# Two-layer decoder trunk on one core: gate columns joined to a key chunk, compression in two steps, other step orders, another order of the first loads

## The chip, the cores and the metric

The kernel runs on one core of a Trainium2 chip. The metric is the device time of one execution in microseconds (us). The core has TensorE (PE in the profile; its weight loads are PEld), VectorE (DVE), ScalarE (ACT), GpSimd (POOL) and SyncE (SP), which here issues most of the DMA transfers. Before the change the median of three runs is 1027.73 us (1026.06 to 1029.51).

## The reference, cut to what matters

256 tokens of width 1024 pass two layers, and each layer is feed-forward, token mixer, feed-forward:

```python
x = x + 0.5 * swiglu(rmsnorm(x, ffn1_norm[i]), ffn1_w_gu[i], ffn1_w_down[i])
h = rmsnorm(x, mix_norm[i])
y = nsa_mixer(h, ...)  # layer 0
y = swa_mixer(h, ...)  # layer 1
x = x + y
x = x + 0.5 * swiglu(rmsnorm(x, ffn2_norm[i]), ffn2_w_gu[i], ffn2_w_down[i])
```

The mixer of layer 0 (called NSA below) projects `h` to 16 query heads, to three pairs of keys and values of 4 groups, and to 48 gate columns (3 branches by 16 heads). The first pair of keys and values is compressed: overlapping blocks of 32 tokens go through a small two-layer network (`w1`, gelu, `w2`) to 15 coarse keys and values. The queries attend to the coarse keys, to selected blocks and to a window, and the three results are added with `sigmoid(gate columns)` as weights. At this size the selected blocks and the window both come to causal attention over all tokens. The mixer of layer 1 (SWA below) is attention over a window of 128 keys with two key groups and a sink per head. Everything is float32.

## The kernel before

**Weights.** Every weight tile is read in pieces of up to 1024 columns (`Weights.load`, line 166): a DMA issue on SP into a tile `raw` (5 buffers, line 172), a rounded copy `hi` (line 173, mostly ACT) and the rest `lo = raw - hi` (line 179; on DVE in one instruction, on POOL in two of 512 columns). `hi` and `lo` have 4 buffers each. A product is then three matmuls (line 119): `hi` by `hi`, `hi` by `lo`, `lo` by `hi`. In the profile the weights of the NSA projection are called nin, those of its output projection nout, of the compression cmp, of SWA sin and sout, of the feed-forward gu and dn; the suffixes `_r`, `_h`, `_l` are raw, hi and lo.

**Which engine.** The table `ENGINES` (line 45) gives for each kind of helper operation a string over A, V and G (ACT, DVE, POOL); the n-th use takes the n-th letter, from the start again after the end (`pick`, line 145).

**Order.** Feed-forward blocks run in the order written. The mixers are made of steps in a written list (`NSA_STEPS`, line 63, and `SWA_STEPS`, line 70). A step named `X01@n` is step X for group 0 and token tile 1; n is added to its priority while it is laid down (`run`, line 139), and the scheduler fills each engine's queue by priority among what is ready, so a negative n pulls a step ahead. The queues themselves run strictly in order. The steps of NSA: `R` is a block of the input projection (`RowsProduct.block`, line 315), for both token tiles or for one (`R00`, `R01`); its accumulator is a PSUM bank of the kind "acc" (two banks), with `+` of the kind "out" and "sc", with `*` of "sc". Chunk x holds the columns of the keys to be compressed, y those of the values, a to d the other keys and values of a group, 0 to 3 the queries, and g the 48 gate columns, which have a block, a weight piece of 384 columns and accumulators of their own (line 699). `K` (line 723) takes x or y through rope and a transpose into `kc`; `B` (line 588) adds the position codes (`xr`) and splits; `H` (line 603) is the whole compression network; `G` (line 706) turns the gate accumulators into gates, one Tanh on ACT (line 710) and one DVE instruction (line 711) per token tile; `P` and `V` prepare queries and keys; `S` is logits and softmax (lines 480 to 512); `M` weighs the values (line 514); `Q` and `L` are the coarse branch. After the list comes nout. SWA has `R`, `A` (keys), `P`, `S`, `M`, and then sout.

**The start** (`Norm.first`, line 263) has an order written by hand: eight matmuls on zeros, loads of the input x on the queues of SP and ACT, of the identity matrix and of all small parameters, transposes of x (`turn`), their eviction with the gain (`leave`, ACT line 203 and DVE line 206), and the first products as their weight pieces come. The scale of the rows (line 237 to 241) is transposed into `rb` (line 391) before the first gate can be worked out.

Of the kernel before, what the change touches and what calls it, by code (L numbers as in the profile page):

```python
# [44 lines left out]
ENGINES = {  # L45
    "hi_gu": "A", "lo_gu": "V", "hi_dn": "A", "lo_dn": "VGVVVGGV", "hi_nin": "AAAAAVAAAAAAVAAA",
    "lo_nin": "VGGGVGGVVVGGVGVG", "hi_cmp": "A", "lo_cmp": "VVGVVVGVVGGVVVGG", "hi_nout": "AAGAAAAVAVGAVAAA",
    "lo_nout": "VG", "hi_sin": "A", "lo_sin": "GGGGGVVVVGGVGVVG", "hi_sout": "A", "lo_sout": "G",
    "sqh": "GAAVAAAGGAAAGGAA", "sql": "GGGVVVGVGGVGVVVG", "qs": "AVVAVAAAAAAAAAAA", "kdh": "VVVAVGGVGVGAAAAA",
    "kdl": "G", "kk": "A", "ropeadd": "GGGVVGGGVGGGVVGG", "sc1": "VVVVVVVVVVVVVAVV", "sc2": "VVVGVVGVVVVVGVVV",  # L50
    "ph": "A", "tmp": "A", "oh": "A", "ol": "VGVVVGVVGVGVVVVV", "dup": "AVVVAVAGAVVVAVVV", "kca": "AVAAAVVA",
    "kcb": "A", "xr": "VGVV", "xhc": "VVVAGVVAVGVVVVVV", "xlc": "GVGGVGGVGVGVVGGV", "pc": "AAVAAAAAVAVAAAAA",
    "late": "GGGVGGGGGGGGGGGG", "xh": "AAAVVVAVAVAVVVAV", "ga": "G", "g0": "A", "u1": "A", "u0": "G", "hv": "V",
    "hh": "AGVAGVGG", "hl": "GGGGVGGV",
}
# [15 lines left out]
    "R0.+ Rk0@10 P01 Rk1@-40 R10+@-30 A1 P00@20 R11 A0@60 S00 P10 S01 P11 S11@-10 R20 S10 R21+@-20 M00@-20 R30 P20 "  # L71
    "S20 R31@-10 M01@-20 P21@-60 S21@80 M10@20 M11 P30@-10 S30@40 M20 M21 M30@-90 P31@10 S31@80 M31@-210"
# [9 lines left out]

IDLE = 8
# [4 lines left out]
NCP = 16  # L88
KCW = 272
# [9 lines left out]
def trunk_kernel(tc, x_in, wgu, wdn, nsa_in, nsa_w1, nsa_out, swa_in, swa_out, small, fgain, consts, out):  # L99
# [3 lines left out]
    with ExitStack() as es:  # L103
# [46 lines left out]
        def copy(key, o, i):  # L150
            c = pick(key)
# [8 lines left out]
        class Weights:  # L160
# [4 lines left out]

            def load(self, c0, n, pieces=None, engines=None):
                o = c0
                for i, w in enumerate(pieces or [PIECE] * (n // PIECE) + [n % PIECE] * (n % PIECE > 0)):
                    raw = wp.tile([P, PIECE], F32, tag="raw", bufs=BUFS["raw"], name=f"{self.name}_r{o}")
                    hi = wp.tile([P, PIECE], F32R, tag="whi", bufs=BUFS["whi"], name=f"{self.name}_h{o}")  # L170
                    lo = wp.tile([P, PIECE], F32R, tag="wlo", bufs=BUFS["wlo"], name=f"{self.name}_l{o}")
                    self.last = nc.sync.dma_start(raw[:, :w], self.src[:, o:o + w]).ins
                    copy("hi_" + self.kind, hi[:, :w], raw[:, :w])
                    letter = engines[i % len(engines)] if engines else pick("lo_" + self.kind)
                    eng = nc.vector if letter == "V" else nc.gpsimd
                    step = 512 if eng is nc.gpsimd else PIECE
                    for q in range(0, w, step):
                        e = min(w, q + step)
                        eng.tensor_tensor(lo[:, q:e], raw[:, q:e], hi[:, q:e], ALU.subtract)  # L179
                    self.parts[o] = (hi, lo)  # L180
                    o += w
# [62 lines left out]
        class Norm:  # L244
# [18 lines left out]
            def first(self, wts, product):  # L263


                def load_x(h, queues):
                    for t, queue in enumerate(queues):
                        queue.dma_start(x[t][h], x_in[t * P:(t + 1) * P, h * 512:(h + 1) * 512])

                evict = {}  # L270

                def turn(*kps):
                    for kp in kps:
                        evict[kp] = transposed(kp, 0, self.h, self.l, self.both, "A")
# [8 lines left out]
                for _ in range(IDLE):  # L283
                    mm(ps, zeros[:, :P], zeros, True, True)
# [12 lines left out]
                turn(2, 3)  # L297
                product(1, 3)
                leave(4, 6)
                wts.load(1024, 1024, [512, 512], "VG")  # L300
                leave(5, 7)
                product(4, 6, 5, 7)
                wts.load(CHUNK, CHUNK, engines="VG")
                for h in range(2):
                    squares(h, h * 512, h * 512 + 512, self.v, True)
                self.r = row_scale(self.v, "n0")


        class RowsProduct:
# [5 lines left out]
            def block(self, ts=(0, 1), tag=None):  # L315
# [52 lines left out]
        def ffn(i, norm, nxt, residual=Residual):  # L368
            with tc.tile_pool(name=f"ffn{i}", bufs=1) as fp:
# [24 lines left out]
                for f in range(NF):  # L394
# [5 lines left out]
                    if i == 0 and f == 3:  # L400
                        with tc.issue_after(wts.last):
                            nc.sync.dma_start(cst[:, P:], consts[:, P:])
                    g0 = fp.tile([P, S], F32, tag="g0", bufs=BUFS["g0"], name=f"g0{f}")
# [147 lines left out]
        def nsa(norm, nxt):  # L551
            with tc.tile_pool(name="nsa", bufs=1) as mp:
# [50 lines left out]
                def compress(xh, xl):  # L603
                    wts1 = Weights(nsa_w1, "cmp")
                    ps = s_bank("hid")[:, :S]
                    for j in range(16):
# [7 lines left out]
                        mm(ps, xlj, wh, False, j == 15)  # L614
                    a = mp.tile([P, P], F32, name="ge_a")
# [9 lines left out]
                    for r, c in own:  # L625
                        nc.vector.tensor_mul(b[r], ps[r, c], a[r])
                    pt = s_bank("hidT")[:, :P]
# [50 lines left out]
                class Finish:  # L678
# [11 lines left out]
                    def scale(self, sm):  # L690
# [8 lines left out]
                                   [48 if c == "g" else S for c in NSA_CHUNKS], "nin",  # L699
                                   ["out" if c == "g" else "acc" for c in NSA_CHUNKS])  # L700
                xh, xl = {}, {}
# [31 lines left out]
                def step_H():  # L733
                    compress(xh, xl)
# [198 lines left out]
def _pack(i):  # L933
# [16 lines left out]
    nsa_blocks.update(g=[(2560, 2608)], x=[(D, D + S)], y=[(D + S, D + 2 * S)])  # L950
# [39 lines left out]
```

## Time and profile before

| what | value |
|---|---|
| median of 3 runs | 1027.73 us (1026.06 to 1029.51) |
| the profiled execution's own time | 1030.59 us |
| its span in the profile | 1028.8 us |
| PE busy over the span | 991.0 us (96%), 5671 matmuls |
| DVE, ACT, POOL busy | 706.0, 554.6, 525.9 us |
| mean granted TensorE clock | 0.982 of full speed |
| HBM read | 167 MB, 163 GB/s over the span |

The span has these stages: start and first feed-forward 0 to 198 us, NSA 198 to 376, two feed-forwards 376 to 745, SWA 745 to 837, last feed-forward to the end. "Busy" of PE is the time in which at least one matmul is in flight, so a PE that is busy can still go at half its clock, which the column PEclk tells (1.00 is 2.4 GHz, 0.50 is 1.2 GHz). A wait is put down to the instruction that ended it.

### The profile page before, as it was taken

To read this page: it belongs to the slowest core of one execution; us is meant where nothing else is said; L and a number is where in the kernel's file an instruction comes from. 1 tells how busy PE (TensorE), PEld (TensorE's weight loads), DVE (VectorE), ACT (ScalarE), POOL (GpSimd) and SP (SyncE) were. 2 spreads that over 40 slices of the span, in tenths; PEclk is the share of its full clock that TensorE was granted. 3 is DMA by queue.
4 is the path that set the end of the run, shared out by engine and by line. 5 is a ranking of instruction groups with operands and counts; after the bars stand their busy time and mean duration, and the time that the engine had idled before them with its cause. 6 is when DMAs were issued, how large, how long until landed. Compare 5 with 4: busy or idle time off the path is not lost.

```text
span 1028.8 us, 15995 instructions
## 1 busy us (share of the span) xinstructions
PE 991.0 (96%) x5671; PEld 858.3 (83%) x5671; DVE 706.0 (69%) x1294; ACT 554.6 (54%) x1041; POOL 525.9 (51%) x503
## 2 busy tenths in 40 slices
PE   7999999998889999999999999999998999999997
PEld 5888888897778788888888888888887778888897
DVE  5777743468878987777535878764177888778533
ACT  5455544347548845555444555544347855555442
POOL 2776563455453316555631465564575516655643
PEclk9999999989989999999999999999999999999999
DMA  7666665542321256666566566656642256666661
GB/s 260 199 202 200 187 190 178 173 143 83 123 83 29 81 159 183 189 190 192 177 195 202 168 203 184 188 166 219 179 142 73 83 164 194 198 185 188 194 188 42
DMA packets 47599, 169.10 MB, mean 164 GB/s; under 512 B 5280, under 2 KB 5792, under 8 KB 47520
## 3 DMA queue, kind: packets, MB, share of 16 engines
q1 hardware_dynamic: 46512, 166.11, 53.9%
q10 hardware_dynamic: 1008, 1.98, 0.6%
q8 instruction: 44, 0.72, 0.3%
q14 instruction: 35, 0.29, 0.1%
HBM read 167.02 MB, written 1.05 MB: 163 GB/s over the span
## 4 chain that ended last, share of the span: by engine, by line
PE 85%; DVE 6%; POOL 3%; ACT 3%; issue 3%; DMA 1%; SPq 0%; POOLq 0%; DVEq 0%; ACTq 0%
PE gu L119 47%; PE dn L119 23%; PE nin L119 5%; PE nout L119 1%; PE sout L119 1%; PE na_o L119 1%; DVE na_p L511 1%; PE sin L119 1%; PE xt L195 1%; ACT sa_p L507 1%; PE sa_o L119 1%; PE na_t L520 1%; DMA gu_r<-in_wgu_dram 1%; POOL sout_l L179 0%; POOL nin_l L179 0%
## 5 line engine op out<-in xcount | busy, mean ns | idle before, releaser
L119 PE MATMUL gu<-xh,gu_h 128*128 128x512 f32 x1408 | 489.2, 393 | 2.4 <-DVE xh L206 2.4
L119 PE MATMUL gu<-xh,gu_l 128*128 128x256 f32 x1408 | 391.7, 280 | 0.2 <-POOL gu_l L179 0.2
L119 PEld LDWEIGHTS gu<-xh,gu_h 128*128 128x128 f32 x1408 | 263.3, 188 | 60.7 <-DVE xh L206 2.6
L119 PEld LDWEIGHTS gu<-xh,gu_l 128*128 128x128 f32 x1408 | 265.5, 189 | 2.3 <-DVE gu_l L179 0.7
L179 DVE TENSOR_TENSOR gu_l<-gu_r,gu_h 128x1024 fp32r<-128x1024 f32 (+1 forms) x175 | 234.0, 1337 | 27.4 <-ACT gu_h L153 26.8
L153 ACT CAST gu_h<-gu_r 128x1024 fp32r<-128x1024 f32 (+2 forms) x178 | 184.6, 1039 | 38.8 <-PE gu L119 16.8
L153 ACT CAST dn_h<-dn_r 128x1024 fp32r<-128x1024 f32 (+1 forms) x89 | 92.2, 1041 | 105.8 <-PE dn L119 99.6
L119 PE MATMUL dn<-dn_h,hh 128*128 128x512 f32 (+1 forms) x396 | 146.0, 369 | 0.0
L119 PE MATMUL dn<-dn_l,hh 128*128 128x512 f32 (+1 forms) x396 | 145.5, 368 | 0.0
L119 PE MATMUL dn<-dn_h,hl 128*128 128x512 f32 (+1 forms) x396 | 145.1, 366 | 0.0
L179 POOL TENSOR_TENSOR dn_l<-dn_r,dn_h 128x512 fp32r<-128x512 f32 x66 | 90.0, 1386 | 100.2 <-ACT dn_h L153 99.9
L179 DVE TENSOR_TENSOR dn_l<-dn_r,dn_h 128x1024 fp32r<-128x1024 f32 (+1 forms) x56 | 71.3, 1277 | 97.9 <-ACT dn_h L153 97.9
L158 POOL TENSOR_TENSOR ga<-g,rb 128x256 f32<-128x256 f32 x88 | 100.3, 1140 | 61.8 <-DVE g L410 52.2
L158 POOL TENSOR_TENSOR hl<-u,hh 128x256 fp32r<-128x256 f32 x66 | 82.4, 1249 | 50.9 <-ACT hh L153 25.1
L158 POOL TENSOR_TENSOR u<-u,rb 128x256 f32<-128x256 f32 x88 | 68.9, 783 | 60.3 <-DVE u L412 60.3
L414 ACT ACTIVATE th<-ga 128x256 f32<-128x256 f32 x88 | 36.9, 419 | 106.7 <-POOL ga L158 106.2
L119 PEld LDWEIGHTS dn<-dn_h,hl 128*128 128x128 f32 x396 | 74.7, 189 | 12.9
L119 PEld LDWEIGHTS dn<-dn_h,hh 128*128 128x128 f32 x396 | 74.8, 189 | 12.4
L119 PEld LDWEIGHTS dn<-dn_l,hh 128*128 128x128 f32 x396 | 74.8, 189 | 11.9
L119 PE MATMUL nin<-nin_h,xh 128*128 128x256 f32 (+1 forms) x352 | 76.0, 310 | 2.0 <-DVE r_b L443 1.9
L153 ACT COPY g<-gu 128x256 f32<-128x256 f32 x88 | 32.8, 373 | 78.0 <-PE gu L119 77.0
L416 DVE SCALAR_TENSOR_TENSOR ga<-th,ga 128x256 f32<-128x256 f32 x88 | 43.1, 490 | 40.1 <-ACT th L414 40.0
(244 smaller groups left out, 1471.7 us busy)
## 6 DMA issues: line engine op xcount, KB each, us to landing
gu_r<-in_wgu_dram SPq DMA_DIRECT2D x174, 512.0 KB, 4.4
dn_r<-in_wdn_dram SPq DMA_DIRECT2D x87, 512.0 KB, 3.8
nin_r<-in_nsa_in_dram SPq DMA_DIRECT2D x20, 512.0 KB, 3.6
sin_r<-in_swa_in_dram SPq DMA_DIRECT2D x10, 512.0 KB, 3.6
nout_r<-in_nsa_out_dram SPq DMA_DIRECT2D x8, 512.0 KB, 3.6
sout_r<-in_swa_out_dram SPq DMA_DIRECT2D x8, 512.0 KB, 3.7
cmp_r<-in_nsa_w_dram SPq DMA_DIRECT2D x4, 512.0 KB, 4.6
x<-in_x_dram ACTq DMA_DIRECT2D x3, 256.0 KB, 6.0
```

What stands on the lines that cost most here:

```text
L119: nc.tensor.matmul(o, w, m, start=start, stop=stop)
L153: nc.scalar.copy(o, i)
L158: (nc.vector if pick(key) == "V" else nc.gpsimd).tensor_tensor(o, a, b, op)
L179: eng.tensor_tensor(lo[:, q:e], raw[:, q:e], hi[:, q:e], ALU.subtract)
L195: nc.tensor.transpose(ps[:, kk * S + t * P:kk * S + (t + 1) * P], x[t][kp // 2][:, c:c + P], ident)
L414: nc.scalar.activation(th, ga, AF.Tanh, scale=0.5)
L416: nc.vector.scalar_tensor_tensor(ga, th, 1.0, ga, ALU.add, ALU.mult)
L507: nc.scalar.activation(o, o, AF.Exp, bias=mn[:, c:c + 1], scale=-1.0, accum_out=sm[:, c:c + 1])
L511: nc.vector.tensor_tensor(o, o, sm[:, b * 4:b * 4 + 4, None].to_broadcast([P, 4, nk]), ALU.mult)
L520: nc.tensor.transpose(ps[:, hh * P:(hh + 1) * P], pr[:, hh, kt * P:(kt + 1) * P], ident)
```

## The change

1. The 48 gate columns are no chunk of their own. They stand behind the 256 columns of chunk x, which so has 304; `G` reads columns 256 to 303 of x's accumulators. The weight pieces of a block whose width does not divide 1024 are whole rows of tiles: x loads 912, 912 and 608 columns in place of 1024, 1024 and, for g, 384.
2. `compress` ends after the matmuls with `w1`; gelu is `compress_rest`, and transpose and second layer are `compress_out`, a new step `I`, which stands after `P11` in the list.
3. Both lists have another order and other offsets.
4. At the start the identity moves from SP's queue to ACT's, the first two weight pieces are issued on SP right after the first part of x, one part of x moves from ACT to SP behind them, only the first 48 columns of the small parameters are loaded there (the other 240 after the fourth block's weights of the first feed-forward, on SP), three more zero matmuls stand between the first transposes and the first product, and evictions and weight splits take another order.
5. Letters in `ENGINES` change. Those that are used, by use:

```
hi_nin  use 5        V -> A   (1024 columns)
hi_nout use 2        G -> A   (8 uses: AAGAAAAV -> AAAAAAAV)
lo_sin  10 uses      GGGGGVVVVG -> GGGVVVGVVG
lo_sout 8 uses       G -> V
xr      use 2        V -> G   (128x512)
xhc     use 2, 3     V, A -> G, A
dup     use 0        A -> V
ol      16 uses      VGVVVGVVGVGVVVVV -> VVVVVGVGGGGGVVVV
sqh 6: A -> G, sql 8: G -> V, kdh 9: V -> A
```

The diff, cut to its core:

```diff
 NSA_STEPS = (
-    "Ry.+@-40 Rx R00* R01 K00@10 K01 K10 Rg.+ Ra P00 G@80 K11 B0@70 V00@50 P01@-70 V01 R10+@-10 B1 S00 R11 S01 "
-    "H@10 M00 P10 Q0@-60 Rb P11 V10 S10 V11 R20@10 R21@170 Rc0 Rc1@-20 P20@100 P21@-40 S11 L00@-400 R30 V21 Q1@-70 "
...
+    "Ry.+@-40 Rx R00* R01@-400 K00@10 K01@-70 K10@60 P00 Ra@-10 B0@70 V00@60 K11@100 P01@-100 B1@-80 G V01 S00@10 S01@70 R10+ R11@190 H M00 P10 Rb@20 P11 I@-10 V10@-210 S10@20 Q0@-50 R20 V11@-50 R21@160 Rc0@-60 ...
 SWA_STEPS = (
-    "R0.+ Rk0@10 P01 Rk1@-40 R10+@-30 A1 P00@20 R11 A0@60 S00 P10 S01 P11 S11@-10 R20 S10 R21+@-20 M00@-20 R30 P20 "
...
+    "Rk0 Rk1@-140 R0.+ A0 R10+ A1 R11@10 P00 R20@-10 P01@-200 S01@-20 S00@-30 P10@30 P11@-100 R21+ P21@130 M00@-10 ...
@@ Norm.first
+                multiply_zeros(8)
                 load_x(0, (nc.sync, nc.scalar))
-                nc.sync.dma_start(ident, consts[:, C_ID:C_ID + P])
-                nc.scalar.dma_start(prm, small)
-                load_x(1, (nc.scalar, nc.scalar))
+                nc.scalar.dma_start(ident, consts[:, C_ID:C_ID + P])
+                raw = [wts.fetch(o, n) for o, n in ((0, 256), (256, 768))]
+                nc.scalar.dma_start(prm[:, :D_SINK], small[:, :D_SINK])
+                load_x(1, (nc.sync, nc.scalar))
+                raw += [wts.fetch(o, 512) for o in (1024, 1536)]
                 nc.scalar.activation(warm, mhalf, AF.Exp)
                 turn(0, 1)
-                wts.load(0, 256, [256], "G")
-                leave(0, 2)
+                multiply_zeros(3)
+                leave(0)
+                wts.split(0, raw[0], 256, "AG")
+                leave(2)
                 product(0)
-                wts.load(256, 768, [768])
+                wts.split(256, raw[1], 768, "AV")
                 leave(1, 3)
...
@@ RowsProduct.block
-                        self.wts.load(c + k * w, n * w)
+                        whole = PIECE // w * w
+                        self.wts.load(c + k * w, n * w, [min(whole, n * w - o) for o in range(0, n * w, whole)])
@@ nsa
-                                   [48 if c == "g" else S for c in NSA_CHUNKS], "nin",
-                                   ["out" if c == "g" else "acc" for c in NSA_CHUNKS])
+                                   [S + GATES if c == "x" else S for c in NSA_CHUNKS], "nin")
...
-                    gacc = accs.pop('g')
+                    gacc = accs["x"]
...
-                        nc.scalar.activation(gv, gacc[t][:, :48], AF.Tanh, scale=rh[:, t:t + 1])
+                        nc.scalar.activation(gv, gacc[t][:, S:S + GATES], AF.Tanh, scale=rh[:, t:t + 1])
...
-                    compress(xh, xl)
+                    hid["b"] = compress_rest(compress(xh, xl))
+
+                def step_I():
+                    compress_out(hid["b"])
```

## Rows read from the trace of the kernel before

**Rows 1.** The page, the span in 40 slices: granted TensorE clock in tenths.

```profile
PEclk9999999989989999999999999999999999999999
```

**Rows 2.** Busy time by stretch of time, whole stages (start, NSA, SWA).

```profile
core 0: us, PE busy (x) PEld busy (x) DVE busy (x) ACT busy (x) POOL busy (x), PEclk, DMA share, GB/s
0.00:25.00 25.00, 19.09 (x90) 13.61 (x91) 13.85 (x27) 14.79 (x27) 6.12 (x10) 0.93 0.79 259
198.00:376.00 178.00, 162.62 (x1058) 143.43 (x1057) 147.33 (x380) 108.55 (x279) 78.10 (x70) 0.93 0.32 95
745.00:837.00 92.00, 82.60 (x532) 72.20 (x531) 71.81 (x178) 60.46 (x151) 49.66 (x55) 0.96 0.38 114
```

**Rows 3.** Busy time by stretch, around the longest low clock in NSA.

```profile
215.90:220.00 4.10, 4.07 (x39) 3.97 (x36) 3.05 (x4) 3.31 (x5) 0.20 (x1) 1.00 0.49 151
220.00:224.90 4.90, 4.90 (x26) 4.90 (x25) 4.78 (x5) 2.30 (x6) 4.82 (x5) 0.50 0.27 94
224.90:230.30 5.40, 5.40 (x27) 5.40 (x27) 2.13 (x4) 1.09 (x2) 3.17 (x3) 0.50 0.16 28
```

**Rows 4.** Waits of PE in NSA, 198 to 376 us: total, times, longest.

```profile
PE nin L119 <- DVE nin_l L179: 4.3, 1, 4.3
PE k_k L469 <- DVE qs L155: 2.3, 1, 2.3
```

**Rows 5.** Busy time by stretch, NSA before and after PE's first wait.

```profile
198.00:238.00 40.00, 39.97 (x300) 39.64 (x298) 28.30 (x52) 19.09 (x32) 20.99 (x21) 0.87 0.38 119
238.00:320.00 82.00, 67.62 (x465) 61.63 (x464) 68.74 (x213) 49.91 (x153) 39.08 (x35) 0.92 0.30 90
```

**Rows 6.** Waits of PE in SWA, 744 to 850 us.

```profile
PE sa_o L119 <- ACT sa_h L153: 4.3, 2, 3.5
PE q_q L458 <- POOL q_sq L158: 2.2, 1, 2.2
```

**Rows 7.** Busy time by stretch, the two holes of SWA.

```profile
757.00:763.00 6.00, 3.81 (x21) 3.61 (x20) 3.45 (x10) 2.57 (x5) 3.58 (x7) 0.72 0.60 175
783.00:790.00 7.00, 3.47 (x17) 2.95 (x17) 4.69 (x16) 2.94 (x12) 2.19 (x4) 0.76 0.40 129
```

**Rows 8.** POOL's queue in order of time, SWA: start, duration, what.

```profile
778.37 3.97 POOL L179 TENSOR_TENSOR sout_l<-sout_r,sout_h 128x512 fp32r<-128x512 f32 x3
782.30 0.73 POOL L158 TENSOR_TENSOR q_a<-q_a,q_b 128x256 f32<-128x256 f32 x1
```

**Rows 9.** The chain that ended last, in order of time, the start.

```profile
1.65 5.55 DMA gu_r<-in_wgu_dram
...
8.58 2.95 PE gu L119 x8
```

**Rows 10.** Waits in the first 26 us.

```profile
PE gu L119 <- DVE xh L206: 2.4, 1, 2.4
PE rb L391 <- DVE n_r L241: 1.8, 1, 1.8
```

**Rows 11.** Groups of instructions by shape, NSA: the gate matmuls (count, busy, mean ns).

```profile
L119 PE MATMUL nin<-nin_h,xh 128*128 128x48 f32 x32 | 7.6, 313 | 0.0
L119 PE MATMUL nin<-nin_l,xh 128*128 128x48 f32 x16 | 5.0, 313 | 0.0
```

**Rows 12.** The chain, NSA: a run of matmuls of 256 columns at full clock.

```profile
200.09 15.71 PE nin L119 x131
```

**Rows 13.** Groups by shape, DVE, 198 to 320 us: busy, mean ns of one.

```profile
L179 DVE TENSOR_TENSOR nin_l<-nin_r,nin_h 128x1024 fp32r<-128x1024 f32 x8 | 11.6, 1451 | 1.7 <-ACT nin_h L153 1.7
L158 DVE TENSOR_TENSOR xr<-kc,prm 128x512 f32<-128x512 f32 x3 | 3.8, 1296 | 1.1 <-ACT kc L153 1.1
```

**Rows 14.** Groups by shape, DVE, 745 to 837 us.

```profile
L179 DVE TENSOR_TENSOR sin_l<-sin_r,sin_h 128x1024 fp32r<-128x1024 f32 x4 | 4.9, 1221 | 2.4 <-ACT sin_h L153 2.4
```

**Rows 15.** ACT's queue in order of time, NSA: a gate's Tanh; the last step of B1.

```profile
224.11 0.30 ACT L710 ACTIVATE gate<-nin,rhalf 128x48 f32<-128x48 f32 x1 [1.00 <-PE nin L119]
...
235.72 0.62 ACT L153 CAST xh<-xr 128x512 fp32r<-128x512 f32 x1 [0.99 <-DVE xr L158]
```

More of the change, by code (lines that the diff above doesn't have):

```diff
@@ L63 @@
 NSA_STEPS = (
[4 rows of a table removed]
+    "Ry.+@-40 Rx R00* R01@-400 K00@10 K01@-70 K10@60 P00 Ra@-10 B0@70 V00@60 K11@100 P01@-100 B1@-80 G V01 S00@10 S01@70 R10+ R11@190 H M00 P10 Rb@20 P11 I@-10 V10@-210 S10@20 Q0@-50 R20 V11@-50 R21@160 Rc0@-60 Rc1@-30 P20@110 S11@-20 L00@-780 P21 Q1@-80 V21 R30@-170 M01 Q2@-60 V20 S20@-170 S21 R31*@150 M11 P30 Rd0@-10 V30@60 M21@30 Rd1@70 M10 P31@30 M20@90 V31@30 S31@-10 S30 Q3@-90 M31@-30 M30"
 )
 SWA_STEPS = (
-    "R0.+ Rk0@10 P01 Rk1@-40 R10+@-30 A1 P00@20 R11 A0@60 S00 P10 S01 P11 S11@-10 R20 S10 R21+@-20 M00@-20 R30 P20 "
@@ L72 @@
-    "S20 R31@-10 M01@-20 P21@-60 S21@80 M10@20 M11 P30@-10 S30@40 M20 M21 M30@-90 P31@10 S31@80 M31@-210"
+    "Rk0 Rk1@-140 R0.+ A0 R10+ A1 R11@10 P00 R20@-10 P01@-200 S01@-20 S00@-30 P10@30 P11@-100 R21+ P21@130 M00@-10 S10 P20 S11@-240 S20 M01@-260 S21 M10 M20 R30 P30@-30 S30@110 M11@90 R31@-30 P31@60 M21 S31 M30 M31@-10"
 )
@@ L81 @@
 TAIL = 8
-IDLE = 8
 EPS = 1e-6
@@ L88 @@
 NCP = 16
+GATES = 3 * NH
 KCW = 272
@@ L148, in pick, with copy @@
             return ENGINES[key][n % len(ENGINES[key])]
-        def copy(key, o, i):
-            c = pick(key)
+        def copy(key, o, i, engine=None):
+            c = engine or pick(key)
             if c == "A":
@@ L164, in __init__, with fetch, split @@
                 self.src, self.name, self.kind, self.parts = src, name, name.rstrip("0123"), {}
+            def fetch(self, o, w):
+                raw = wp.tile([P, PIECE], F32, tag="raw", bufs=BUFS["raw"], name=f"{self.name}_r{o}")
+                self.last = nc.sync.dma_start(raw[:, :w], self.src[:, o:o + w]).ins
+                return raw
+            def split(self, o, raw, w, engines=None):
+                hi = wp.tile([P, PIECE], F32R, tag="whi", bufs=BUFS["whi"], name=f"{self.name}_h{o}")
+                lo = wp.tile([P, PIECE], F32R, tag="wlo", bufs=BUFS["wlo"], name=f"{self.name}_l{o}")
+                copy("hi_" + self.kind, hi[:, :w], raw[:, :w], engines and engines[0])
+                eng = nc.vector if (engines[1] if engines else pick("lo_" + self.kind)) == "V" else nc.gpsimd
+                step = 512 if eng is nc.gpsimd else PIECE
+                for q in range(0, w, step):
+                    e = min(w, q + step)
+                    eng.tensor_tensor(lo[:, q:e], raw[:, q:e], hi[:, q:e], ALU.subtract)
+                self.parts[o] = (hi, lo)
             def load(self, c0, n, pieces=None, engines=None):
@@ L168, in load @@
                 for i, w in enumerate(pieces or [PIECE] * (n // PIECE) + [n % PIECE] * (n % PIECE > 0)):
[L169 to L180, printed above, removed]
+                    self.split(o, self.fetch(o, w), w, engines and "A" + engines[i])
                     o += w
@@ L282, in first, with multiply_zeros @@
                 ps = s_bank("idle")
-                for _ in range(IDLE):
-                    mm(ps, zeros[:, :P], zeros, True, True)
+                def multiply_zeros(n):
+                    for _ in range(n):
+                        mm(ps, zeros[:, :P], zeros, True, True)
+                multiply_zeros(8)
                 load_x(0, (nc.sync, nc.scalar))
-                nc.sync.dma_start(ident, consts[:, C_ID:C_ID + P])
-                nc.scalar.dma_start(prm, small)
-                load_x(1, (nc.scalar, nc.scalar))
+                nc.scalar.dma_start(ident, consts[:, C_ID:C_ID + P])
[3 more added lines that the diff above has]
+                raw += [wts.fetch(o, 512) for o in (1024, 1536)]
                 nc.scalar.activation(warm, mhalf, AF.Exp)
                 turn(0, 1)
-                wts.load(0, 256, [256], "G")
-                leave(0, 2)
+                multiply_zeros(3)
+                leave(0)
+                wts.split(0, raw[0], 256, "AG")
+                leave(2)
                 product(0)
-                wts.load(256, 768, [768])
+                wts.split(256, raw[1], 768, "AV")
                 leave(1, 3)
@@ L298, in first @@
                 product(1, 3)
-                leave(4, 6)
-                wts.load(1024, 1024, [512, 512], "VG")
-                leave(5, 7)
+                leave(4)
+                wts.split(1024, raw[2], 512, "AV")
+                wts.split(1536, raw[3], 512, "GG")
+                leave(6, 5, 7)
                 product(4, 6, 5, 7)
@@ L614, in compress, with compress_rest @@
                         mm(ps, xlj, wh, False, j == 15)
+                    return ps
+                def compress_rest(ps):
                     a = mp.tile([P, P], F32, name="ge_a")
@@ L626, in compress, with compress_out @@
                         nc.vector.tensor_mul(b[r], ps[r, c], a[r])
+                    return b
+                def compress_out(b):
                     pt = s_bank("hidT")[:, :P]
```

17 lines of the change are left out of this document (4 added, 13 removed), and 2 rows, old and new, of the table NSA_STEPS.

## The prediction

> **What bounds the kernel now.** I read the clock of the 40 slices first, then whole stages, then PE's waits, then the stretches around them. The clock row shows full speed almost everywhere, with dips at the start, in NSA and once in SWA [rows 1]; the four feed-forwards and their projections run dense at 2.4 GHz, and the change touches no step of theirs. What can move is in three stages [rows 2]: the start (25 us), NSA (178 us) and SWA (92 us), 295 us together.
>
> NSA has two halves. From 198 to 238 us PE is never idle, but its mean clock is only 0.87, and DVE is busy 28.3 of 40 us [rows 5]. The loss sits in one place: from 220.0 to 230.3 us the clock is 0.50 while PE is busy every moment [rows 3]. Just before, from 215.9 us, PE had worked on the gate chunk: 48 matmuls of 48 columns [rows 11]. No wait stands before this dip. From 238 to 320 us PE has 67.6 of 82 us, and DVE 68.7 [rows 5]; PE's longest waits there, 4.3 and 2.3 us, are both for DVE [rows 4]. So the first half is bound by PE, the second by an order in which DVE is late.
>
> SWA is dense but for two holes, each followed by a half clock [rows 7]: 2.2 us for a query split on POOL, and 3.5 us (of 4.3) for a weighting that needs ACT [rows 6]. Ahead of the second, POOL has spent 3.97 us on splits of sout, and the rope sum of the next queries stands behind them in its queue [rows 8].
>
> At the start the first product begins at 8.58 us, after the first weight piece, issued at 1.65 us, has taken 5.55 us to land [rows 9]. PE waits 2.4 us there, and 1.8 us more at the end for the row scale [rows 10].
>
> **The change part by part.**
>
> *Gate columns.* Removed are 48 narrow matmuls. At full clock 39 matmuls of that stretch take 4.10 us, 0.105 us each [rows 3], so 48 take 5.0 us; that pitch barely depends on the width, for 131 matmuls of 256 columns take 15.71 us, 0.120 each [rows 12]. Added are 48 columns to 48 matmuls that exist anyway: in proportion to width 0.120 x 48/256 = 0.0225 us each, 1.1 us in all (nothing at best). The clock comes on top. In the two stretches at 0.50, 26 matmuls take 4.90 us where 0.105 each would be 2.7, and 27 take 5.40 where 0.120 each would be 3.2: 4.4 us lost. If the narrow matmuls brought the dip, PE gains 5.0 - 1.1 + 4.4 = 8.3 us by 238 us; if they did not, 3.9 us. I take 8.3, because this is the dip with no idle time before it and the narrow matmuls are what came before.
>
> The Trainium skill ("TensorE: Matmul & The Clock Gate", section "Why this matters for your kernels") would have a fall of the clock in mid-kernel come from an idle gap between bursts of matmuls. By that rule the 4.4 us stay lost and the join is worth 3.9 us; here no idle time stands before the fall, so the row speaks against the rule in this place.
>
> *What of it lasts.* At 238 us DVE must be as far as before. It has 28.3 us of work there; in the later half it runs at 68.7/82 = 84%, and 28.3/0.84 = 33.7 us is 6.3 us less than 40. So about 6.3 us of the 8.3 pass without another relief. Letters take some off DVE: one of the compression's sums goes to POOL (1.30 us [rows 13]), and of the projection's splits one of 1.45 us [rows 13] leaves and one of 608 columns comes, by width 0.86; the other letters of this stretch (two casts away, a copy added) are shorter than that sum, -0.9 us together as an estimate. That makes -2.8 us of DVE, of which I count the part that lies after PE's first wait as 1.2. NSA: -6.3 - 1.2 = **-7.5 us**.
>
> *Compression in two steps, other NSA order.* No instruction is added or removed by the cut of `H`; the transpose, second layer and their evictions on PE, ACT and DVE come behind `P11`. PE waits on no step of the compression among the long waits [rows 4], so by itself I cost it at nothing; its cover is the queries' work that now stands ahead of it, and if that cover is gone the coarse branch is late, which only the last steps need. The reordering of the rest can take away or repeat the two long waits: bounds -6.6 and +6.6 us, and since neither end is nearer, 0.
>
> *Weight pieces.* x has three issues on SP in place of two, g's is gone: three and three, the same bytes. Both pieces of query chunk 0 now split on POOL, ahead of POOL's rope sums; PE needs them only after x, 48 matmuls later (6.8 us at 0.142), which covers it. Without that cover it costs one POOL split, about two of 1.3 us [rows 8].
>
> *SWA.* The holes cost 2.2 + 3.5 us of waiting and, by clock, 6 x 0.28 + 7 x 0.24 = 3.4 us: 9.1 us at most. The second (5.2) goes, since sout's splits leave POOL's queue; of the first (3.9) I count half, as one split of the early chunks fewer is on POOL and keys come ahead of queries. What is late next is DVE: eight splits of sout at 1.22 us each [rows 14] are 9.8 us, one of sin 1.22 more, against 71.8 of 92 us [rows 2]: 90% busy. A third of the 9.8, 3.2 us, I count on the path (bounds 0 and 9.8, nearer to 0 because 20 us are free). SWA: -5.2 - 1.95 + 3.2 = **-4.0 us**.
>
> *Start.* The first weight piece is issued one place earlier on SP, the eviction of x comes before the cast, and 120 KB of parameters leave the first transfers. Bounds: the whole wait of 2.4 us and the clock's 25 x 0.07 = 1.7 us below; nothing above, if the row scale at the end, where PE waits 1.8 us, decides alone. Extra zero matmuls fall into that wait of 2.4 us; the part of x that moved behind weights is needed only after two products. I take **-1.0 us**. The late parameters (one more issue on SP) and the gates' unchanged two Tanh and two DVE instructions cost nothing: both lie beside dense matmuls.
>
> Sum: -7.5 - 4.0 - 1.0 = -12.5 us. The profiled execution, 1030.59 us, stands 2.9 us over the median; its terms carry over, so 1027.7 - 12.5 = **1015.2 us**.
>
> **The rivals.** *(a) The dip stays* or wanders to another place: NSA -3.9 x 0.76 (what lasts of 8.3) = -3.0, SWA and start as above: 1019.7 us. The skill's rule makes this; for it speaks that dips follow the holes of SWA [rows 7], against it that PE was busy all along [rows 3]. Chance 0.17.
>
> *(b) DVE takes it all back.* NSA's gain waits at the next late DVE instruction, so that only DVE's 2.8 us count, and sout's splits cost SWA their 9.8 against the 9.1 of the holes; the start is hidden behind the row scale: -2.8 + 0.7 = -2.1, 1025.6 us, and within 0.3% (3.1 us) of before. For it speaks DVE's share of 80% in NSA [rows 2], against it its idle 11.7 us before 238 [rows 5]. Chance 0.15.
>
> *(c) Gates hold the banks: slower.* x's two "acc" banks are now free only when `G` has read them, and `G` stands behind `B1`; `R01` and `Ra` need those banks. Before, the Tanh came at 224.1 us, and B1's last step ended at 236.3 [rows 15]. If the queue of ACT keeps the listed order, PE stops after the first half of chunk 0, about 213 us (x's end at 210.1, plus 24 x 0.120), until 236.3: 23.3 us, and 1.7 more at half clock; less the 8.3 gained that is +16.7, with SWA -4.0 and start -1.0: 1039.4 us. It decides from the point where the Tanh comes more than some 12 us after PE could have gone on. Against it: ACT is busy only 19.1 of 40 us there [rows 5], and a Tanh that is ready can be laid down ahead. Chance 0.08.
>
> That the change does not do what it says is hardly possible for the gate chunk; for the step lists it is case (b).
>
> **How the numbers follow.** Forecast 0.60, (a) 0.17, (b) 0.15, (c) 0.08. A difference under 0.3% cannot be told from none here. The forecast's own range comes from its unknowns, reorder 6.6, start 2.4, SWA 5 either way, which seldom add: 1004 to 1025. Downwards 1004 leaves out about 1 in 10; upwards I go to 1028 to take in (a) and (b) and leave out (c) and little else. Faster: nearly all of the forecast, (a) and a fourth of (b): 0.78. Same: 0.11. Slower: (c) and some of the reorder: 0.11.
>
> **What would show it.** Right: no clock of 0.50 in NSA without an idle PE before it; matmuls of 304 columns at about 0.14 us; PE's first wait in NSA some 6 us earlier; no sout split on POOL and no hole of 3.5 us in SWA; first product before 8 us. Wrong: a dense PE at 0.50 again, a Tanh of the gates that PE waits for, DVE over 90% in SWA with PE waiting for sout's splits, or holes as long as before in other places.

## The result, and the profile after

The changed kernel takes 1017.06 us (median of 4 runs, 1015.64 to 1018.57); beside it the kernel before takes 1028.62 us (4 runs). The ratio is 0.9887, 95% interval 0.9861 to 0.9914: 1.1% faster, 1.9 us above the forecast and inside its range. The profiled run took 1016.99 us over a span of 1014.9 us.

The clock row of the changed kernel's page, the row that answers [rows 1], has one dip left, over two slices in NSA:

```profile
PEclk9999999998899999999999999999999999999999
```

Busy time by stretch of time in the changed kernel, the start and then NSA and SWA from first to last matmul, to be held against [rows 2]; then the rows that answer [rows 3, 5]:

```profile
core 0: us, PE busy (x) PEld busy (x) DVE busy (x) ACT busy (x) POOL busy (x), PEclk, DMA share, GB/s
0.00:25.00 25.00, 19.54 (x100) 13.97 (x101) 15.34 (x30) 14.27 (x27) 7.18 (x12) 1.00 0.83 279
198.30:366.50 168.20, 154.65 (x1012) 134.92 (x1011) 134.02 (x379) 110.44 (x279) 75.38 (x73) 0.96 0.34 104
736.00:822.40 86.40, 79.98 (x529) 69.14 (x527) 72.42 (x186) 59.96 (x151) 25.65 (x37) 1.00 0.39 120
224.10:226.20 2.10, 0.05 (x2) 0.00 (x1) 2.10 (x4) 1.01 (x3) 2.02 (x3) 1.00 0.26 105
226.60:230.10 3.50, 3.50 (x20) 3.50 (x19) 3.09 (x5) 1.00 (x3) 2.58 (x3) 0.52 0.02 5
198.30:238.00 39.70, 37.23 (x283) 35.84 (x281) 27.74 (x59) 21.54 (x34) 25.60 (x25) 0.96 0.51 158
```

In the table below the stages are cut exactly: NSA was 178.3 us and is 168.2, SWA was 91.3 and is 86.4, and the time up to the first down matmul was 136.0 and is 136.8. That is -10.1 - 4.9 + 0.8 = -14.2 us; the profiled executions differ by 13.6, and everything else is equal within 0.5. The medians differ by 11.6 only: the profiled execution of before, 1030.59 us, was 2.0 us over its median, so a stage of that one profile is somewhat long. The gain lies where the prediction put it, in other shares: NSA gave more, the start cost something. In NSA the dense dip is gone: the fall to half clock at 226.7 us now follows an idle TensorE (0.05 of 2.1 us busy). Half clock is not gone from NSA. Four stretches of 3.4 us are left (from 226.7, 243.8, 254.0 and 267.7 us), each behind waits of TensorE (2.05 us ahead of the first, 1.9 ahead of the second, shorter ones ahead of the others); before had four like these and the dense one of 10.2 us. SWA runs at full clock throughout.

TensorE's waits in the changed kernel, the first two lines from NSA, the others from SWA and from the first 26 us (total, times, longest), against [rows 4, 6, 10]:

```profile
PE r_q L460 <- POOL r_sq L144: 3.2, 2, 2.0
PE hid L105 <- DVE na_mx L502: 1.9, 1, 1.9
...
PE sa_o L105 <- ACT sa_h L139: 1.8, 2, 1.3
PE sa_o L105 <- ACT sa_p L509: 1.3, 1, 1.3
...
PE rb L392 <- DVE n_r L232: 2.5, 1, 2.5
PE gu L105 <- ACT xh L194: 0.8, 1, 0.8
```

Of the waits of before, 4.3 us for a split weight in NSA and 3.5 us for a weighting in SWA have gone; the new longest one in NSA is 2.0 us, for GpSimd's part of a query split (r_sq). In GpSimd's queue a weight split, which before came behind the rope sum of these queries (225.87 us after 219.79), now stands ahead of it (219.21 before 222.04), and in e1 below, which has the join alone, it does so too. At the start the wait ahead of the first product fell from 2.4 to 0.8 us, and the wait for the row scale rose from 1.8 to 2.5.

### The profile page after: what moved, and what is told of

The parts are those of the page before. It is cut to its first block, busy times and chain, and to the rows that moved or that the text cites. A ratio compares the mean times of both kernels' runs of the same rounds, so it can differ in the third digit from the quotient of the medians.

```text
span 1014.9 us, 15910 instructions
## 1 busy us (share of the span) xinstructions
PE 982.3 (97%) x5626; PEld 845.8 (83%) x5626; DVE 694.0 (68%) x1299; ACT 556.3 (55%) x1041; POOL 493.5 (49%) x490
## 5 line engine op out<-in xcount | busy, mean ns | idle before, releaser
L139 ACT CAST gu_h<-gu_r 128x1024 fp32r<-128x1024 f32 (+1 forms) x177 | 184.1, 1042 | 45.6 <-PE gu L105 26.3
L144 POOL TENSOR_TENSOR ga<-g,rb 128x256 f32<-128x256 f32 x88 | 96.0, 1091 | 62.3 <-DVE g L412 57.9
L416 ACT ACTIVATE th<-ga 128x256 f32<-128x256 f32 x88 | 36.8, 418 | 91.3 <-POOL ga L144 90.5
L105 PE MATMUL nin<-nin_h,xh 128*128 128x256 f32 (+1 forms) x320 | 65.4, 297 | 1.8 <-DVE r_b L445 1.6
```

The source lines that it names most:

```text
L105: nc.tensor.matmul(o, w, m, start=start, stop=stop)
L144: (nc.vector if pick(key) == "V" else nc.gpsimd).tensor_tensor(o, a, b, op)
L416: nc.scalar.activation(th, ga, AF.Tanh, scale=0.5)
```

## The experiments

The table sets the profiled executions side by side; ratios and intervals are to the kernel before on the same chip. "Start" ends at the first down matmul; "idle" is NSA's length less TensorE's busy time, "clock" its mean granted clock, both from the busy time by stretch. "gu" counts the matmul rows between 45 and 130 us, a stretch of the first feed-forward in which no wait stands.

| kernel | median us | ratio | start | NSA | idle | clock | SWA | gu |
|---|---|---|---|---|---|---|---|---|
| before | 1028.62 | 1 | 136.0 | 178.3 | 15.4 | 0.93 | 91.3 | 492 |
| changed | 1017.06 | 0.9887 (0.9861 to 0.9914) | 136.8 | 168.2 | 13.6 | 0.96 | 86.4 | 484 |
| e1 join only | 1022.42 | 0.9937 (0.9919 to 0.9955) | 136.5 | 170.9 | 16.2 | 0.96 | 90.3 | 493 |
| e2 gates wide | 1029.63 | 1.0010 (0.9995 to 1.0025) | 136.7 | 177.0 | 16.5 | 0.95 | 90.9 | 492 |
| e3 no join | 1018.20 | 0.9904 (0.9884 to 0.9923) | 139.7 | 169.2 | 11.5 | 0.97 | 86.4 | 483 |
| e4 start only | 1028.54 | 0.9986 (0.9967 to 1.0006) | 137.1 | 176.5 | 17.0 | 0.95 | 89.7 | 492 |
| e5 row scale late | 1017.48 | 0.9881 (0.9855 to 0.9907) | 138.4 | 166.2 | 14.7 | 0.98 | 86.4 | 492 |
| e6 no zeros | 1017.79 | 0.9871 (0.9843 to 0.9899) | 138.9 | 165.1 | 14.7 | 0.99 | 86.5 | 483 |
| e7 sout on POOL | 1021.68 | 0.9912 (0.9883 to 0.9942) | 138.9 | 165.7 | 13.8 | 0.98 | 88.6 | 483 |
| e8 one step | 1020.52 | 0.9906 (0.9883 to 0.9928) | 138.1 | 169.5 | 16.1 | 0.97 | 86.5 | 483 |
| e9 lists only | 1040.90 | 1.0107 (1.0083 to 1.0132) | 136.5 | 186.0 | 17.7 | 0.89 | 93.7 | 492 |
| e10 letters only | 1026.37 | 0.9978 (0.9963 to 0.9993) | 136.4 | 179.4 | 19.9 | 0.95 | 84.9 | 492 |
| e11 sout on DVE | 1025.04 | 0.9973 (0.9956 to 0.9990) | 135.1 | 176.4 | 15.4 | 0.94 | 88.3 | 492 |
| e12 old start | 1013.88 | 0.9854 (0.9827 to 0.9880) | 137.2 | 167.6 | 14.6 | 0.97 | 86.4 | 493 |

One profile is not a stage's length for good. NSA's program is the same in the changed kernel, e5, e6, e7 and e12, and took 168.2, 166.2, 165.1, 165.7 and 167.6 us (mean 166.6); in before, e4 and e11 it took 178.3, 176.5 and 176.4 (mean 177.1). A difference under some 3 us between two profiles of NSA says nothing. SWA's program is the same in before, e1, e2 and e4: 91.3, 90.3, 90.9 and 89.7 us (mean 90.6); the changed one took 86.4 or 86.5 in six kernels. Where a text below subtracts from before's single profile, the difference from these means stands beside it.

### Does the join pay, and do narrow matmuls bring the dense dip? (e1, e2, e3)

**e1**: the join alone, on the kernel before.

```diff
-    "Ry.+@-40 Rx R00* R01 K00@10 K01 K10 Rg.+ Ra P00 G@80
+    "Ry.+@-40 Rx R00* R01 K00@10 K01 K10 Ra P00 G@80
...
-    nsa_blocks.update(g=[(2560, 2608)], x=[(D, D + S)],
+    nsa_blocks.update(x=[(D, D + S), (2560, 2608)],
```

> The kernel before with the gates' 48 columns joined to x and nothing else of the change (same step lists without the gate step, same letters, same start). Theory A (the narrow matmuls bring the dense half clock): no clock of 0.50 with a busy PE between 215 and 235 us, PE 8.3 us ahead at the end of the first key-and-value chunk; of NSA's length (178.3 us from the first projection matmul to the last of the output product) about 6 us go: 172 us, ratio about 0.994. Theory B (the clock does not depend on the gate matmuls): a stretch of some 10 us at 0.50 stays there or a little later, NSA loses 3 us or less: ratio 0.997 or more. Theory C (the other step order, not the join, won NSA): ratio 1.000, the gain is taken back at the next wait for VectorE.

**e2**: the gate chunk stays apart but is padded to 256 columns.

```diff
-                                   [48 if c == "g" else S for c in NSA_CHUNKS], "nin",
+                                   [S] * len(NSA_CHUNKS), "nin",
...
-    nsa_blocks.update(g=[(2560, 2608)],
+    nsa_blocks.update(g=[(2560, 2608), (0, S - 48)],
```

> The kernel before with the gate chunk apart as it was, but padded to 256 columns: 208 columns of the first query weights are multiplied beside the gates and read by nobody, so the matmuls of this chunk are as wide as the rest. Theory A (narrow matmuls bring the dense half clock): these 48 matmuls cost 48 x 0.015 = 0.7 us more, the half clock from 220 to 230 us is gone and gives 4.4 us back: TensorE 3.7 us ahead at 238 us, NSA about 2 to 3 us shorter, ratio about 0.997. Theory B: the half clock stays with these wide matmuls, NSA 0.7 us longer at most, ratio 1.000 to 1.001.

**e3**: the changed kernel with the gates in a chunk of their own again.

```diff
-    "Ry.+@-40 Rx R00* R01@-400 K00@10 K01@-70 K10@60 P00
+    "Ry.+@-40 Rx R00* R01@-400 K00@10 K01@-70 K10@60 Rg.+ P00
...
-    nsa_blocks.update(x=[(D, D + S), (2560, 2560 + GATES)],
+    nsa_blocks.update(g=[(2560, 2560 + GATES)], x=[(D, D + S)],
```

> The changed kernel with the gates taken out of x again: a chunk of 48 columns of its own, multiplied behind the second key rope step, as before. Theory A: the dense half clock comes back behind the 48 narrow matmuls, TensorE loses 8.3 us by 238 us, and NSA grows from 168.2 us to about 174 us: ratio to the kernel before about 0.994. Theory B: no dense half clock, NSA 3 to 4 us longer than in the changed kernel, ratio about 0.992. Theory C (order and letters did it all): NSA stays at 168 to 169 us, ratio 0.989.

Busy time by stretch (columns as above) around the place of the dip in e2, where the gate matmuls are wide:

```profile
216.00:221.00 5.00, 4.90 (x41) 4.56 (x40) 3.70 (x5) 3.55 (x6) 0.48 (x1) 1.00 0.55 175
221.00:226.00 5.00, 5.00 (x45) 5.00 (x44) 4.93 (x5) 4.22 (x7) 4.92 (x5) 1.00 0.23 83
```

The same view of e3, narrow again, in the changed order:

```profile
215.00:224.00 9.00, 8.97 (x78) 8.78 (x77) 6.37 (x10) 4.42 (x6) 1.37 (x3) 0.99 0.55 181
224.00:227.40 3.40, 3.40 (x18) 3.40 (x17) 3.13 (x3) 0.13 (x1) 3.32 (x4) 0.50 0.33 119
227.40:230.70 3.30, 3.30 (x17) 3.30 (x17) 1.98 (x3) 2.48 (x5) 3.30 (x3) 0.50 0.00 0
```

The clock part of theory A is shown. In e2 the clock is 1.00 with a dense TensorE; in e3, at a place where the changed kernel has none, the dip stands in a dense TensorE. e4, e9, e10 and e11, which keep the narrow chunk, have it too (from 221.8, 220.9, 221.9 and 220.8 us), so with before that makes all six kernels with narrow gate matmuls, and the eight others do not have this dip. It begins while the narrow matmuls are still running: in before they run from 216.0 to 224.3 us, and the clock falls at 220.0.

What the clock is worth is another matter. e1 behaves as expected: NSA 7.4 us shorter (6.2 against the mean), ratio 0.9937. But e2, which wins back the dense dip too, gains 1.3 us of NSA in its profile (0.1 against the mean) and nothing in time: it has one 10.2 us stretch of half clock later, from 265.6 us behind a wait, where before has 3.4 us. Its clock over the whole of NSA, 0.95, is that of e4, which has the dense dip; and e3, which has it, stands at 0.97, within the 0.96 to 0.99 of the five kernels with the changed NSA. So the dip can be taken away, but that NSA's clock rises by it as a whole is not shown. And in the changed order the join is worth 169.2 - 166.6 = 2.6 us of NSA, by one profile of e3 against the mean above, and 1.7 us by the ratios, whose intervals overlap, though e3 has 48 matmuls more. Part of the work saved there turns into waiting: e3 idles 11.5 us and the changed kernel 13.6.

### Lists or letters? (e9, e10)

**e9**: both new step lists, the gates apart, the compression in two steps; letters and start of before. **e10**: the new letters alone.

```diff
-    "R0.+ Rk0@10 P01 Rk1@-40 R10+@-30 A1 P00@20 R11 A0@60
+    "Rk0 Rk1@-140 R0.+ A0 R10+ A1 R11@10 P00 R20@-10 P01@-200
...
```

```diff
-    "lo_nout": "VG", "hi_sin": "A", "lo_sin": "GGGGGVVVVGGVGVVG", "hi_sout": "A", "lo_sout": "G",
+    'lo_nout': 'VG', 'hi_sin': 'A', 'lo_sin': 'GGGVVVGVVGGVGVVG', 'hi_sout': 'A', 'lo_sout': 'V',
...
```

> The kernel before with the new step lists of NSA and SWA and the compression in two steps, the gates still a chunk of their own, the old letters and the old start. In the changed kernel without the join, new lists and new letters together brought NSA from 178.2 to 169.2 us. Theory H (the lists do it): NSA 168 to 171 us here, SWA 86 to 88 us, ratio 0.990 to 0.992. Theory I (the letters do it): NSA 176 us or more, SWA 90 to 91 us, ratio 0.997 to 1.000.

> The kernel before with the new letters of the engines and nothing else. Theory H: NSA 176 to 179 us, SWA shorter by the 2 us at most that sout's splits gave in the changed kernel, ratio 0.997 to 1.002 (the letters were drawn up for another order). Theory I: NSA 170 to 172 us, SWA 87 us, ratio 0.990 to 0.992.

Neither theory holds for NSA. The lists alone make it 7.7 us longer, the letters alone 1.1 longer, and both together (e3, with the new start) make it 9.1 shorter; against the mean of 177.1 us these are 8.9 and 2.3 longer and 7.9 shorter. For SWA the letters alone give all and more, by one profile: 84.9 us. The new list in addition costs 1.5 (86.4), and with the old letters 2.4 (93.7; 3.1 against the mean). A stretch and the longest wait of e9's NSA show how a good list fails with the wrong letters:

```profile
258.50:285.80 27.30, 20.99 (x86) 17.50 (x87) 16.43 (x53) 9.95 (x32) 6.66 (x6) 0.50 0.33 97
...
PE na_o L115 <- DVE na_l L520: 4.1, 1, 4.1
```

TensorE stands 4.1 us for VectorE's low half of the probabilities, until 260.6 us, and from 258.5 us on the clock is at half for 27.3 us, 6.3 of them idle: the last 2.1 us of that wait and further ones (1.2 us for ScalarE, 1.2 for GpSimd among them). In e3, with the same lists, that wait and that stretch are missing. So here the letters decide whether a step's inputs stand ready when its turn in the list comes; e3 has the new start as well, but that lies 200 us earlier and alone left NSA as it was (e4).

### SWA's second hole (e7, e11)

```diff
-... 'hi_sout': 'A', 'lo_sout': 'V', ...
+... 'hi_sout': 'A', 'lo_sout': 'G', ...
```

That is **e7**, on the changed kernel; **e11** is the reverse on the kernel before.

> The changed kernel with the low halves of sout's weights split on GpSimd again, all else as changed. Theory F (the splits on GpSimd, ahead of the queries' rope sums, made the second hole of SWA): a wait of about 3.5 us and a half clock come back before the output product, and eight 1.22 us splits leave VectorE: SWA 86.4 us becomes 88 to 91 us, ratio 0.991 to 0.993. Theory G (the new step order took the hole away): SWA stays at 86 us or gets shorter as VectorE has 9.8 us less to do, ratio 0.986 to 0.989.

> The kernel before with the low halves of sout's weights on VectorE and nothing else. By the prediction the second hole of SWA (5.2 us with its clock) goes and 3.2 us come back on VectorE: SWA 91.2 us becomes 89 us, ratio 0.998. Rival: with the old order the queries' rope sums are late on VectorE instead, SWA 91 us or longer, ratio 1.000 to 1.003.

SWA's waits in e11, then the two longest in e7:

```profile
PE q_q L458 <- POOL q_sq L158: 3.4, 2, 2.2
PE sout L119 <- ACT swa_oh L153: 1.9, 2, 1.0
PE sa_o L119 <- ACT sa_h L153: 1.8, 2, 1.0
...
PE q_q L460 <- DVE q_sq L144: 1.9, 1, 1.9
PE sa_o L105 <- ACT sa_h L139: 1.4, 2, 1.2
```

Theory F holds in direction and at its lower end: the splits on GpSimd cost SWA 88.6 - 86.4 = 2.2 us in the new order, 91.3 - 88.3 = 3.0 in the old one (2.3 against the mean), by one profile each. The hole it names does not come back, though: the longest wait in e7 is 1.9 us, for a query split on VectorE, and the weighting's is 1.2 us; e9, with the new list and the old letters, has no wait over 1.9 us in SWA either. So the 3.5 us hole needs the old order as well as the splits on GpSimd. In e11 the wait of 3.5 us for the weighting [rows 6] is down to 1.0, and the query split's 2.2 us stay, as the prediction had it; in e10, where that split's letters changed as well, the wait for it is 0.6. By the ratios e7 lies 2.6 us over the changed kernel, and the intervals overlap; in its profile the last feed-forward is longer too, which is told below.

### The compression in one step (e8)

```diff
-                    hid["b"] = compress_rest(compress(xh, xl))
-
-                def step_I():
-                    compress_out(hid["b"])
+                    compress_out(compress_rest(compress(xh, xl)))
```

> The changed kernel with the compression in one step again at its first place. Prediction: the cut is worth nothing, NSA 168.2 us within 1 us, ratio 0.9887. Rival: TensorE then stands at the compression's transpose until VectorE and ScalarE have done the activation between the two halves: a wait of 1.5 to 3 us at about 256 us with a half clock behind it, NSA 170 to 172 us, ratio 0.991 to 0.992.

```profile
PE hidT L636 <- DVE ge_b L631: 1.7, 1, 1.7
```

The rival's wait appears, in this line of TensorE's waits in NSA: the transpose stands for VectorE's product, and idle time is 16.1 us against 13.6 to 14.7 in the five profiles of the two-step program. NSA is 169.5 us against their mean of 166.6, and the ratio stands for 2.0 us more; the intervals overlap, so the cut is worth something between nothing and 3 us, with a wait of 1.7 us shown (0.3 in the changed kernel). It is not e8's longest: the wait for VectorE's r_b is 2.9 us there, 1.6 in the changed kernel.

### The start (e4, e5, e6, e12)

**e4** has the new start alone on the kernel before; **e12** the old start on the changed kernel; **e6** leaves out the three zero matmuls; **e5** puts the row scale's transposes later. The core of e4 (e12 is its reverse), then e6, then e5:

```diff
+                raw = [wts.fetch(o, n) for o, n in ((0, 256), (256, 768))]
+                nc.scalar.dma_start(prm[:, :D_SINK], small[:, :D_SINK])
+                load_x(1, (nc.sync, nc.scalar))
...
-                multiply_zeros(3)
...
+                with later(100 if i == 0 else 0):
                     for t in range(NT):
                         nc.tensor.transpose(ps[:, t * P:(t + 1) * P], ...
```

> The kernel before with only the start of the change (order of the first loads, three zero matmuls more, splits on the listed engines, most parameters later). In the changed kernel the first product began 0.5 us earlier and the row scale was ready 1.55 us earlier, yet the end of the first gate and up stage came 0.8 us later. Theory D (the start costs: the row scale's transposes stand earlier in TensorE's queue and wait 2.5 us, and this whole stage runs at 0.236 us per 512-column matmul in place of 0.230): first down matmul at 136.8 us, ratio 1.001. Theory E (the slower pitch was of that execution or chip, not of the start): 0.230 us again, first down matmul 1 to 2 us before 136.0, ratio 0.998 to 0.999.

> The changed kernel with the transposes of the row scale (and their copy) placed some 34 matmuls later in TensorE's queue, behind the third block of gate and up columns of the first feed-forward. Theory D (the changed start's gain is lost because these transposes stand early and TensorE waits 2.5 us for VectorE's row scale): the wait of 2.5 us near 20.5 us is gone, the first down matmul comes 2 to 2.5 us earlier, ratio about 0.987 where the changed kernel has 0.9887. Theory E (the stage's end is set elsewhere: weights land late or VectorE is behind): the wait moves to another instruction, ratio 0.9887 again.

> The changed kernel without its three additional zero matmuls at the start. If they keep the clock up: a stretch at 0.50 comes back near 8 us and the first gate and up stage ends 1 to 1.7 us later, ratio 0.990. If they only fill a wait: the same first product at 8 us, no half clock, ratio 0.9887.

> The changed kernel with the start of before (order of the first loads, no additional zero matmuls, all parameters at once). If the new start is worth nothing: ratio 0.988 as the changed kernel has it. If it is worth the 1 us of the prediction: 0.990. In the first gate and up stage 0.236 us per 512-column matmul would show that this slower pitch goes with the later stages' letters and lists, 0.230 that it needs the new start as well; at 0.230 the first down matmul comes at 136 us and the ratio is 0.986 to 0.987.

e5's wait moves, as theory E had it: the row scale no longer stops TensorE, but the first evictions that need it, which now come later on the other engines, do:

```profile
PE gu L105 <- DVE u L415: 2.7, 1, 2.7
```

e6 has half clock back (5.7 us of TensorE's work at 0.50 from 8.0 us); its time does not differ. Its first product begins at 9.1 us, 1 us later than in the changed kernel, but e3 and e8, which have the zeros, begin theirs at 9.4 and 9.3 us. What the start as a whole is worth shows best in e12: with the old start the changed kernel takes 1013.88 us, 3.2 less than with the new one; the two intervals overlap. The profiles agree in sign: with the old start (before, e1, e2, e9, e10, e11, e12) the first down matmul comes at 135.1 to 137.2 us, mean 136.3; with the new one as written (the changed kernel, e3, e4, e7, e8) at 136.8 to 139.7, mean 138.1. The new start costs 1.8 us by these means; the times alone do not prove it, and e4's ratio of 0.9986 shows no loss without the rest of the change.

Most of that is a slower pitch of the same matmuls. Busy time by stretch, 45 to 130 us, in before:

```profile
45.00:130.00 85.00, 85.00 (x492) 74.92 (x491) 66.06 (x103) 47.48 (x81) 53.47 (x51) 1.00 0.66 195
```

In the changed kernel:

```profile
45.00:130.00 85.00, 85.00 (x484) 73.77 (x483) 64.50 (x101) 47.48 (x80) 48.20 (x50) 1.00 0.64 189
```

And in e12:

```profile
45.00:130.00 85.00, 85.00 (x493) 74.95 (x492) 65.76 (x102) 47.58 (x82) 54.37 (x52) 1.00 0.65 193
```

Full clock and no idle time in all three, yet 484 matmuls in place of 492 or 493: 1.4 us less work done in 85 us. In the median a 512-column matmul takes 0.236 us from its start to the next one's start, against 0.230. It is so in the five kernels that have the new start, the row scale early and the new lists and letters; e4 (new start, old lists and letters) and e5 are at 492. So the slower pitch goes with the new start and the rest of the change together, and e12 does not have it.

## Why the prediction was right, and where its steps failed

*The time* came out within 2 us in part by luck. Held against the means of the profiles, NSA gave 10.5 us where 7.5 were said, SWA 4.2 where 4.0 were said, and the start cost 1.8 where 1.0 was to be gained: two errors of some 3 us, opposite in sign. The readings of before have two slips that change no sum: [rows 1] shows two dips, both in NSA (those of start and SWA stand in [rows 2] as 0.93 and 0.96), and VectorE's share of NSA there is 83%, not 80.

*The gate columns* held in sum: 6.3 us of NSA were predicted to last, and e1 gives 7.4 (6.2 against the mean). TensorE's price of the join is 0.9 us for 48 matmuls (predicted 1.1), for 18 of them lie between these two starts, 0.139 us each:

```profile
208.94 0.30 PE L105 MATMUL nin<-nin_l,xh 128*128 128x304 f32 x1
...
211.45 0.30 PE L105 MATMUL nin<-nin_l,xh 128*128 128x304 f32 x1
```

That the narrow matmuls brought the dense dip is shown by e1 to e3. That its 4.4 us come back as time is not: e2 has the dip away and gains nothing. What is left of the gain was worked out from VectorE's pace, yet TensorE's first long wait is now for GpSimd; so the agreement of 6.3 with e1 is partly luck too.

The Trainium skill ("TensorE: Matmul & The Clock Gate", section "Why this matters for your kernels") would have the clock fall from an idle gap between bursts of matmuls. By that rule the dip of 220.0 us would have stayed, and the trace differs in this place (idle before it 0.03 us in six kernels); the changed kernel's fall at 226.7 us does follow a gap, of 2.05 us. Rival (a) falls in its mechanism, though in e2 half clock does turn up in another place. Its price does not fall: in the changed order the join brought 2.6 us, near the 3.0 that (a) gave it.

*The order of NSA at 0* is the step that failed, with "the compression split at nothing" beside it. Lists and letters together, without the join, gave 9.1 us (e3; 7.9 against the mean), beyond the 6.6 that stood as the bound. The letters' 1.2 us do not explain it, since alone they gave nothing (e10). With them in place the join adds 2.6. The prediction added a join of 6.3 to an order of 0; they overlap, and 10.1 came out where 7.5 was said. The split's cover, "the queries' work that now stands ahead of it", is there, but without it there is a wait of 1.7 us (e8). In before this wait is not among those of 0.2 us or more; once the join lets TensorE come earlier it shows in the old order as well (1.2 us in e1).

*SWA*, -4.0 predicted, -4.9 measured (-4.2 by the means), held in sum. Sout's splits were to give -5.2 + 3.2 = -2.0; moving them gave -2.2 and -3.0 (e7, e11), but no run shows the 3.2 us on VectorE by themselves, and with the new order the 3.5 us hole is gone without sout's letter too (e7). The rest was put at -1.95 for half of the first hole and is 86.4 - 88.3 = -1.9, but from other parts: the other letters' -3.4 (84.9 less 88.3) and the new list's +1.5. That it fits so closely is luck.

*The start* is mis-signed: -1.0 predicted, +0.8 in the profile and +1.8 by the means. In the changed kernel's profile the first product came 0.5 us earlier (8.05 us), the half clock went, and TensorE begins 100 instructions in the first 25 us where before had 90 [rows 2], 3 of them zeros. Other profiles do not bear that out as the work of the new start: with it as written (the changed kernel, e3, e4, e7, e8) the first product begins at 8.05 to 9.36 us, mean 8.9; with the old one (seven kernels) at 7.94 to 8.87, mean 8.4. In the first 26 us the new start is ahead by 3 matmuls in the mean, 0.5 us, while the old one alone scatters from 88 to 101, and the mean clock there is 0.87 to 1.00 with the old start, 0.96 to 1.00 with the new. The slower pitch of the following 110 us then takes more than that. The step that failed is that matmuls which the change does not touch were taken to keep their pace; the trace of before could not show it.

Rival (b) is refuted by e1 alone, rival (c) by the changed trace: the Tanh came at 213.8 and 216.3 us, and TensorE's weight load waited 0.2 us for it:

```profile
L717 ACT ACTIVATE gate<-nin,rhalf x2: 300/300/300, 213.8 to 216.3; 128x48 f32<-128x48 f32 x2
```

Of the signs named beforehand three came true (no dense dip, the width's price, no sout split on GpSimd with no 3.5 us hole), and the first product missed its 8 us by 0.05. TensorE's first long wait in NSA ended at 226.2 us where that of before ended at 242.6, 16 us earlier and not 6, and for another instruction, GpSimd's r_sq. It comes with the join, for e1 has it at 225.8 us.

## What to carry to other kernels

Step order and engine assignment are one choice: in NSA each of them alone was worth nothing or less, together some 8 to 9 us, so test a schedule whole and don't add the worth of parts that shorten the same stage. Narrow matmuls can cost more than their time, since a dense run of them took the clock down with no idle time; join them to wider ones, but ask what the stretch waits for next, as the clock alone gave no time back in e2. And take a change apart once it is measured: the new start, the part that looked harmless, cost 1.8 us of what the others had won by the profiles, and the version without it (e12, 1013.88 us) has the lowest time here, though its interval overlaps that of the changed kernel; the changed letters with SWA's old list (84.9 against 86.4 us) would be the next to try, and were not tried together.

## What the hardware showed that was not expected

The same idle gap does not always bring the clock down. In the five profiles with the same NSA program TensorE waits 2.05 or 2.06 us for the same instruction, GpSimd's r_sq. In the changed kernel half clock follows (the row from 226.60 us above), as in e7 and e12; in e6, and in e5, it does not. e6, the gap and what follows:

```profile
226.10:228.20 2.10, 0.10 (x1) 0.00 (x0) 2.10 (x4) 1.07 (x3) 2.02 (x4) 1.00 0.19 76
228.20:231.70 3.50, 3.44 (x29) 3.45 (x30) 3.47 (x6) 1.95 (x3) 3.06 (x4) 1.00 0.02 5
```

29 matmuls against 20 in 3.5 us. NSA's mean clock in these five lies between 0.96 and 0.99, and its length between 165.1 and 168.2 us, the longest at the lowest clock and the shortest at the highest.

The slower pitch is not tied to the first stage. The last feed-forward of e7 has it, and that of the changed kernel does not; the same 80 us in e7 and then in the changed kernel:

```profile
860.00:940.00 80.00, 80.00 (x455) 69.31 (x454) 59.37 (x93) 45.09 (x76) 42.33 (x47) 1.00 0.58 185
```

```profile
860.00:940.00 80.00, 80.00 (x463) 69.98 (x463) 62.48 (x96) 45.46 (x76) 43.51 (x48) 1.00 0.65 190
```

There it costs 2.4 us over the stage (187.3 us from SWA's last matmul to the last of all in place of 184.9). e9's last feed-forward has it as well. In the first stage, e4 and the changed kernel have the same instructions in the same order on TensorE, VectorE, ScalarE and GpSimd up to 125 us, and still differ, 492 against 484; so the stage's order alone does not make it. In the changed kernel it holds from 30 to 130 us (115 or 116 matmuls in every 20 us, 117 in before). What sets it stays open; no run here tells whether it hangs on the moment at which the last wait ends, on addresses, or on where the program lies.
